# One ordered list instead of two for the head and the first feed-forward of a macaron block

## The chip, the cores and the metric

The kernel runs on one core of a Trainium2 chip. The core has a matrix engine (TensorE, PE in the profile), a vector engine (VectorE, DVE), a scalar engine (ScalarE, ACT), GpSimd (POOL) and SyncE (SP), which issues most of the transfers. The metric is the device time of one execution in microseconds (us), the median of several.

## The reference

One block on 256 tokens of width 2048, all in float32: a SwiGLU feed-forward (width 5632), a mixer, and a second feed-forward, each with an RMS norm before and after it and a residual.

```python
def _swiglu(x, w_gate, w_up, w_down):
    return (jax.nn.silu(x @ w_gate) * (x @ w_up)) @ w_down
...
f = _swiglu(_rmsnorm(h, ln_ffn1_pre[l]), ffn1_gate[l], ffn1_up[l], ffn1_down[l])
h = h + MACARON_WEIGHT * _rmsnorm(f, ln_ffn1_post[l])
mx = _hybrid_mixer(_rmsnorm(h, ln_mix_pre[l]), w_in[l], ...)
h = h + _rmsnorm(mx, ln_mix_post[l])
f = _swiglu(_rmsnorm(h, ln_ffn2_pre[l]), ffn2_gate[l], ffn2_up[l], ffn2_down[l])
h = h + MACARON_WEIGHT * _rmsnorm(f, ln_ffn2_post[l])
```

The mixer projects its input by `w_in`, runs an RWKV-7 recurrence on one part and windowed means on another (`_pool_branch`, with small matrices `pool_w`), gates both and projects by `w_out`.

## The kernel before

**Products.** Every float32 product is made of three: each operand is split into a high half (a cast to fp32r) and a low half (the operand less its high half). `mm3` (L332 to L334) issues the three matmuls, high with high (named L332 in the profile), low with high, high with low. A weight tile of 128x1024 goes from DRAM into a buffer (SP), is cast to its high half `wH` on ACT (L308, L386, L639), and its low half `wL` is a subtraction on DVE (L309, L396, L644). High and low halves sit in rings of five buffers each, so DVE and ACT stay a few tiles ahead of PE. Other tiles come from a common pool of 33 buffers (`unit`).

**The head.** `head` is the start of the program: it loads the input x in 512-column pieces and the first 512 columns of the gate's weights, transposes x on PE (`tr`, L939), and makes the high half `xH` of the transposed input on ACT (L948) and its low half `xL` on DVE (L957). Its loop over 16 blocks k of the contraction does two `mm3` for each k (token halves 0 and 1, banks `mm_120` and `mm_121`), and at every second k turns the next piece of x and splits the next weight tile.

**The first feed-forward's list.** What follows, the rest of `ffn`, is collected in `Plan`: each operation is a node with an engine, a cost and its dependencies. `Plan.solve` orders the nodes by these costs, and `run` issues them in that order. It begins with `normed` (four joins of `xH` and `xL` to `nx`, L1249, then a scaling by the norm's factor and a new split) and the up-projection's first 512 columns (`fetch`, with the cast at L386 and the low half at L396).

**Who sets the order.** `manual_schedule` opens a list: what is issued inside it, on the engines named, keeps its order. `head` opens one for PE, ACT, DVE and SP; `run` opens one for these and POOL. Between two lists, and outside any, a scheduler that estimates times (`schedule_with_timeline_sim=True`) decides what goes first on an engine. The mixer's recurrence and its pool branch are such code: generators paced by `yield` and placed by that scheduler.

**The mixer, as far as it matters here.** `rwkv` runs twice, on two halves of the channels. For the first half: `shift` (L1502 on ACT, L1505 on DVE) mixes a token with the one before it (`zr`, with a scratch `zb`); transposes `pV` on PE and their copies (L1823, L1824 on ACT); transposes `pk` (L1831) and a product on DVE (L1832); `AR` and `BK`, operands of the recurrence, from L1857 to L1867 on DVE; and `pA` (L1881), the matmuls of `BK` with `AR`. In the names below `R` is one of 15 work tiles. `pool_mix` makes the small products `mc` (L901) with `pool_w`, evicted to `yb` (L1710 on ACT, L1711 on DVE). Between them stand the large products with `w_in`, which need their weight halves from L308 and L309.

Of the kernel before, what the change touches and what calls it, by code (L numbers as in the profile page):

```python
# [76 lines left out]
class Tok:  # L77


    def __init__(s, *res):  # L80
        s.res, s.of, s.left, s.end, s.n = res, None, 0, 0.0, 1
# [150 lines left out]
class Block:  # L232
    def __init__(s, tc, ctx):
        s.tc = tc
        s.nc = nc = tc.nc
        E = ctx.enter_context
        s.n = 0
        s.nxt = None
        s.late, s.after, s.chain_pow = [], [], None
        s.own_stats = False  # L240
        s.plan, s.ready = Plan(), {}
        s.cp = E(tc.tile_pool(name="cp", bufs=1))
        s.wp = E(tc.tile_pool(name="wp", bufs=3))
        s.up = E(tc.tile_pool(name="up", bufs=NUNITS))
        s.tp = E(tc.tile_pool(name="tp", bufs=TB))
        s.sp = E(tc.tile_pool(name="sp", bufs=4))
        s.dp = E(tc.tile_pool(name="dp", bufs=1, space=bass.MemoryType.DRAM))
        s.pm = E(tc.tile_pool(name="pm", bufs=4, space=PSUM))
        s.pt = E(tc.tile_pool(name="pt", bufs=4, space=PSUM))
        s.ident = s.const([P, P], "ident")  # L250
        make_identity(nc, s.ident)
        s.mhalf = s.const([P, 16], "mhalf")
        nc.gpsimd.memset(s.mhalf, -0.5)
# [22 lines left out]

    def run(s):

        E = mybir.EngineType
        with s.tc.manual_schedule(engines={E.PE, E.Activation, E.DVE, E.SP, E.Pool}):
            for n in s.plan.solve():
                n.fn()
            if not s.own_stats:
                s.stats()
        s.plan, s.ready = Plan(), {}
# [506 lines left out]
    def head(s, w, c0, KT, do, keep, xs):  # L794

        load, turn = xs
        w32 = {}

        def get(k, n):
            w32[k] = (n, s.get_w(w, k, n, c0, 512, own=True))  # L800

        def split(k):
            n, t = w32[k]
            keep(s.two(t, k, n, 512))
        E = mybir.EngineType
        with s.tc.manual_schedule(engines={E.PE, E.Activation, E.DVE, E.SP}):
            ps = s.psum("warm")
            for _ in range(WARM):
                s.nc.tensor.transpose(ps[:, :P], s.ident, s.ident)
            load(0, 0)  # L810
            load(1, 0)
            load(None, None)
            get(0, 1)
            get(1, 1)
            get(2, 1)
            get(3, 1)
            for c in range(1, 4):
                load(0, c)
                get(4 * c, 2)
                load(1, c)  # L820
                get(4 * c + 2, 2)
            split(0)
            turn(0, 0)
            split(1)
            turn(1, 0)
            split(2)
            split(3)
            for k in range(KT):
                do(k, 0)
                do(k, 1)  # L830
                if k % 2 == 0 and k + 4 < KT:
                    turn(k // 2 % 2, k // 4 + 1)
                    split(k + 4)

    def stats(s):
        while s.late:
            for f in s.late.pop(0):
                f()
# [123 lines left out]
    def turn(s, T1, h, src):  # L962

        dst = T1.rearrange("p (j h k c) -> p h k j c", j=4, h=2, k=4)[:, h]
        s.nc.vector.transpose(out=dst, in_=src.rearrange("p (k j c) -> p k j c", k=4, j=4))  # L965
# [1197 lines left out]
```

## Time and profile before

| | |
|---|---|
| median of 3 runs | 2007.45 us (2005.02 to 2007.62) |
| profiled execution | 2005.37 us, span 2003.7 us |
| busy in the span | PE 1990.0 us, DVE 1813.6, ACT 1224.3, POOL 410.0 |
| granted TensorE clock | 0.999 |
| moved | 472.36 MB, 236 GB/s in the mean |

The span runs from the first to the last instruction. In a timeline row the first number is the start, the second the duration, both in us; then come engine, line of the kernel, operation, output and inputs, shapes and count; a bracket gives the idle time in front of it on its engine and what ended that. Durations of matmuls that follow each other overlap, so their pace is read from the starts. A row of the waits gives the sum in us, the number of times and the longest. SPq is SP's queue of transfers. A row of stretches gives the length, the busy time of PE, weight loads, DVE, ACT and POOL with counts, then the granted clock, the share of the DMA engines and GB/s.

### The profile page before, as it was taken

What the parts mean: (1) busy time and instruction counts of PE and PEld (TensorE: products, weight loads), DVE (VectorE), ACT (ScalarE), POOL (GpSimd) and SP (SyncE); (2) the same over time, 40 slices, a digit from 0 to 9 for tenths busy, and PEclk for the clock granted to TensorE, in tenths of its full rate; (3) what the DMA queues carried; (4) which work ended last, traced back from release to release, by engine and by line L of the source; (5) the groups of instructions that cost most, each with busy time, mean ns of one, the idle gap of its engine ahead of it and who ended that gap; (6) DMA issues with size and microseconds to landing.
All of it is one profiled execution on the core that took longest, in us unless ns stands there. A gap on an engine that the chain in (4) does not pass through costs nothing.

```text
span 2003.7 us, 29050 instructions
## 1 busy us (share of the span) xinstructions
PE 1990.0 (99%) x9903; PEld 1644.7 (82%) x9903; DVE 1813.6 (91%) x2462; ACT 1224.3 (61%) x1631; POOL 410.0 (20%) x747
## 2 busy tenths in 40 slices
PE   9999999999999999999999999999999999999998
PEld 7888888888888888888788788888888888888886
DVE  6999999999999957799689678989999999999997
ACT  7566665676665566685466434575666656666563
POOL 2222231323000113412320111012222313230000
PEclk9999999999999999999999999999999999999999
DMA  9788798878778767757556547768888988876784
GB/s 341 226 268 270 216 304 271 254 238 257 211 229 272 264 191 210 206 174 219 147 168 189 169 158 262 263 226 276 265 269 254 276 259 244 258 242 207 232 284 158
DMA packets 253941, 472.36 MB, mean 236 GB/s; under 512 B 27363, under 2 KB 30816, under 8 KB 253792
## 3 DMA queue, kind: packets, MB, share of 16 engines
q1 hardware_dynamic: 213984, 400.89, 60.4%
q0 software_dynamic: 39520, 69.08, 15.3%
q8 instruction: 78, 1.28, 0.3%
q10 hardware_dynamic: 288, 0.52, 0.1%
q14 instruction: 71, 0.58, 0.1%
HBM read 445.45 MB, written 8.39 MB: 227 GB/s over the span
## 4 chain that ended last, share of the span: by engine, by line
PE 93%; DVE 3%; DMA 2%; issue 1%; ACT 0%; SPq 0%; DVEq 0%; POOLq 0%; POOL 0%; ACTq 0%
PE mm L332 25%; PE mm L334 24%; PE mm L333 24%; PE ms L333 5%; PE ms L334 5%; PE ms L332 5%; DMA w<-in_ffn_down_dram 1%; DVE wL L644 1%; PE tr L939 1%; DVE wL L396 1%; DMA w<-in_w_out_dram 0%; PE pA L1881 0%; DVE t L622 0%; PE mc L901 0%; DVE t L627 0%
## 5 line engine op out<-in xcount | busy, mean ns | idle before, releaser
L332 PE MATMUL mm<-wH,xH 128*128 128x512 f32 (+1 forms) x2008 | 784.3, 391 | 2.0 <-ACT wH L386 1.5
L334 PE MATMUL mm<-wH,xL 128*128 128x512 f32 (+1 forms) x2008 | 779.4, 388 | 0.1
L333 PE MATMUL mm<-wL,xH 128*128 128x512 f32 (+1 forms) x2008 | 779.3, 388 | 0.1
L332 PEld LDWEIGHTS mm<-wH,xH 128*128 128x128 f32 x2008 | 377.2, 188 | 80.9 <-ACT wH L386 1.9
L334 PEld LDWEIGHTS mm<-wH,xL 128*128 128x128 f32 x2008 | 377.0, 188 | 78.7 <-DVE xL L957 1.1
L333 PEld LDWEIGHTS mm<-wL,xH 128*128 128x128 f32 x2008 | 377.3, 188 | 75.7 <-DVE wL L309 0.4
L639 ACT CAST wH<-t 128x1024 fp32r<-128x1024 f32 x244 | 257.1, 1055 | 221.2 <-PE mm L334 121.0
L386 ACT CAST wH<-w 128x1024 fp32r<-128x1024 f32 x293 | 302.8, 1053 | 128.6 <-PE mm L334 100.8
L396 DVE TENSOR_TENSOR wL<-w,wH 128x1024 fp32r<-128x1024 f32 x293 | 351.9, 1227 | 13.8 <-ACT wH L386 12.5
L644 DVE TENSOR_TENSOR wL<-t,wH 128x1024 fp32r<-128x1024 f32 x244 | 295.7, 1234 | 10.9 <-ACT wH L639 10.2
L309 DVE TENSOR_TENSOR wL<-w,wH 128x1024 fp32r<-128x1024 f32 (+2 forms) x184 | 217.5, 1190 | 84.6 <-ACT wH L308 83.2
L308 ACT CAST wH<-w 128x1024 fp32r<-128x1024 f32 (+2 forms) x184 | 188.8, 1030 | 167.0 <-PE mm L334 147.5
L639 ACT CAST wH<-w 128x1024 fp32r<-128x1024 f32 x244 | 200.1, 837 | 109.7 <-PE mm L334 75.1
L982 POOL DMA_DIRECT2D x<-T x352 | 180.6, 608 | 389.6 <-DVE T L965 76.1
L644 DVE TENSOR_TENSOR wL<-w,wH 128x1024 fp32r<-128x1024 f32 x244 | 231.6, 966 | 0.9 <-ACT wH L639 0.9
L333 PE MATMUL ms<-wL,sH 128*128 128x512 f32 x312 | 121.5, 389 | 0.2 <-DVE wL L644 0.2
L332 PE MATMUL ms<-wH,sH 128*128 128x512 f32 x312 | 121.4, 389 | 0.0
L334 PE MATMUL ms<-wH,sL 128*128 128x512 f32 x312 | 121.4, 389 | 0.0
L617 POOL DMA_DIRECT2D t<-in_ffn_up_dram x48 | 59.8, 1256 | 230.8 <-DMA t<-in_ffn_up_dram 56.1
L631 DVE TENSOR_TENSOR t<-w,t 128x512 f32<-128x512 f32 x122 | 85.5, 701 | 0.5 <-DMA w<-in_ffn_down_dram 0.2
L627 DVE TENSOR_TENSOR t<-w,t 128x512 f32<-128x512 f32 x122 | 85.3, 700 | 0.3 <-DMA w<-in_ffn_down_dram 0.3
L622 DVE TENSOR_TENSOR t<-w,w 128x1024 f32<-128x1024 f32 x60 | 73.8, 1231 | 2.8 <-DMA w<-in_ffn_down_dram 2.8
(353 smaller groups left out, 2312.4 us busy)
## 6 DMA issues: line engine op xcount, KB each, us to landing
w<-in_w_in_dram SPq DMA_DIRECT2D x128, 512.0 KB, 4.3
w<-in_ffn_down_dram SPq DMA_DIRECT2D x104, 512.0 KB, 6.5
w<-in_ffn_up_dram SPq DMA_DIRECT2D x94, 512.0 KB, 6.0
w<-in_ffn_gate_dram SPq DMA_DIRECT2D x92, 512.0 KB, 6.6
w<-in_ffn_gate_dram SPq DMA_DIRECT2D x168, 256.0 KB, 5.5
w<-in_ffn_down_dram SPq DMA_DIRECT2D x130, 256.0 KB, 4.9
w<-in_ffn_up_dram SPq DMA_DIRECT2D x116, 256.0 KB, 5.9
t<-in_ffn_up_dram POOLq DMA_DIRECT2D x48, 512.0 KB, 8.4
```

The costliest lines, as they stand in the source:

```text
L308: s.nc.scalar.copy(vH, v)
L309: s.nc.vector.tensor_tensor(out=vL, in0=v, in1=vH.bitcast(F32), op=ALU.subtract)
L332: nc.tensor.matmul(ps, aH, bH, start=start, stop=False, skip_group_check=seeded)
L333: nc.tensor.matmul(ps, aH, bL, start=False, stop=False, skip_group_check=seeded)
L334: nc.tensor.matmul(ps, aL, bH, start=False, stop=stop, skip_group_check=seeded)
L386: nc.scalar.copy(x["H"], x["v"])
L396: nc.vector.tensor_tensor(out=x["L"], in0=x["v"], in1=x["H"].bitcast(F32), op=ALU.subtract)
L627: V.tensor_tensor(out=v["t24"][:, 0], in0=v["a"][:, 0], in1=v["t13"][:, 1], op=ALU.add)
L631: V.tensor_tensor(out=v["t24"][:, 1], in0=v["b"][:, 1], in1=v["t24"][:, 0], op=ALU.add)
L639: nc.scalar.copy(H, src)
L644: V.tensor_tensor(out=L, in0=src, in1=H.bitcast(F32), op=ALU.subtract)
L982: nc.gpsimd.dma_start(out=x[0][q * 32:q * 32 + 32, i], in_=src[i * 32:i * 32 + 32, q])
```

## The change

The list that `head` opens is not closed at its end. It is kept in `s.open`, and `run` goes on in it; where no list is open, `run` opens one as before. Both now name the same five engines, so POOL is in the head's list too. No operation is added, removed or altered.

```diff
-        s.plan, s.ready = Plan(), {}
+        s.plan, s.ready, s.open = Plan(), {}, None
...
+    def listed(s):
+        E = mybir.EngineType
+        return s.tc.manual_schedule(engines={E.PE, E.Activation, E.DVE, E.SP, E.Pool})
+
     def run(s):
 
-        E = mybir.EngineType
-        with s.tc.manual_schedule(engines={E.PE, E.Activation, E.DVE, E.SP, E.Pool}):
+        with s.open or s.listed():
+            s.open = None
             for n in s.plan.solve():
                 n.fn()
...
-        E = mybir.EngineType
-        with s.tc.manual_schedule(engines={E.PE, E.Activation, E.DVE, E.SP}):
+        stack = ExitStack()
+        stack.enter_context(s.listed())
+        with stack:
             ps = s.psum("warm")
...
+            s.open = stack.pop_all()
```

In the changed kernel the lines behind `__init__` stand 4 lower, those behind `head` 6 lower (L332 is L336, L957 is L963), and buffer numbers are smaller by 3. Apart from that the order of instructions differs in two places; SP's and POOL's is the same throughout, and so is PE's outside the first place.

**First place: the seam of the two lists, PE.** `mm_120` and `mm_121` are the head's banks, `mm_498` (now `mm_495`) is the up-projection's. Before, near the end of the head:

```order
L334 MATMUL mm_121<-wH_317,xL_96 128x512
L332 MATMUL mm_120<-wH_346,xH_97 128x512
L332 MATMUL mm_498<-wH_488,xH_91 128x512
L333 MATMUL mm_120<-wL_347,xH_97 128x512
L334 MATMUL mm_120<-wH_346,xL_98 128x512
L332 MATMUL mm_121<-wH_346,xH_97 128x512
```

And in the changed kernel, 24 rows later, at the head's end:

```order
L338 MATMUL mm_120<-wH_375,xL_98 128x512
L336 MATMUL mm_121<-wH_375,xH_97 128x512
L337 MATMUL mm_121<-wL_376,xH_97 128x512
L338 MATMUL mm_121<-wH_375,xL_98 128x512
L336 MATMUL mm_495<-wH_485,xH_91 128x512
L337 MATMUL mm_495<-wL_486,xH_91 128x512
L338 MATMUL mm_495<-wH_485,xL_92 128x512
```

The up-projection's first matmul stood among the head's; it now stands behind all of them, followed by its second.

**The same seam, DVE.** `wL_318` to `wL_376` are the head's weight low halves, `xL` the input's, `nx` the joins, `wL_489` (now `wL_486`) the up-projection's first low half. Before:

```order
L309 TENSOR_TENSOR wL_318<-w_45_161,wH_317 128x1024
L957 SCALAR_TENSOR_TENSOR xL_98<-tr_333,g_90,xH_97 128x128 x4
L1249 TENSOR_TENSOR nx_457<-xH_93,xL_94 128x1024
L1249 TENSOR_TENSOR nx_465<-xH_95,xL_96 128x1024
L1249 TENSOR_TENSOR nx_473<-xH_91,xL_92 128x1024
L309 TENSOR_TENSOR wL_347<-w_46_164,wH_346 128x1024
L957 SCALAR_TENSOR_TENSOR xL_98<-tr_362,g_90,xH_97 128x128 x4
L309 TENSOR_TENSOR wL_376<-w_47_167,wH_375 128x1024
L1249 TENSOR_TENSOR nx_481<-xH_97,xL_98 128x1024
L396 TENSOR_TENSOR wL_489<-w_121_459,wH_488 128x1024
```

Changed:

```order
L313 TENSOR_TENSOR wL_318<-w_45_161,wH_317 128x1024
L963 SCALAR_TENSOR_TENSOR xL_98<-tr_333,g_90,xH_97 128x128 x4
L313 TENSOR_TENSOR wL_347<-w_46_164,wH_346 128x1024
L963 SCALAR_TENSOR_TENSOR xL_98<-tr_362,g_90,xH_97 128x128 x4
L313 TENSOR_TENSOR wL_376<-w_47_167,wH_375 128x1024
L1255 TENSOR_TENSOR nx_454<-xH_93,xL_94 128x1024
L1255 TENSOR_TENSOR nx_462<-xH_95,xL_96 128x1024
L1255 TENSOR_TENSOR nx_470<-xH_91,xL_92 128x1024
L1255 TENSOR_TENSOR nx_478<-xH_97,xL_98 128x1024
L400 TENSOR_TENSOR wL_486<-w_121_456,wH_485 128x1024
```

Three joins went from ahead of the head's last two weight low halves to behind them. ACT's order at the seam is the same in both.

**Second place: the mixer's first half, ACT**, about 855 to 895 us into the span. Before:

```order
L308 CAST wH_8489<-w_1803_8487 128x512
L1502 ACTIVATE zb<-R_6933,cols_724 128x256
L1502 ACTIVATE zr_8002<-R_6933,omu 128x256
L1502 ACTIVATE zb<-R_6933,cols_724 128x256
L1502 ACTIVATE zr_8002<-R_6933,omu 128x256 x3
L1783 ACTIVATE R_6932<-R_6935 128x1024
L1870 CAST yH_6963<-ident 128x1
L308 CAST wH_8509<-w_1808_8507 128x512
L1824 COPY R_6945<-pV_8375 64x4x64
L1823 COPY R_6944<-pV_8375 64x4x64
L1823 COPY R_6944<-pV_8380 64x4x64
L1824 COPY R_6945<-pV_8380 64x4x64
```

Changed:

```order
L312 CAST wH_8486<-w_1803_8484 128x512
L312 CAST wH_8506<-w_1808_8504 128x512
L1830 COPY R_6942<-pV_8372 64x4x64
L1829 COPY R_6941<-pV_8372 64x4x64
L1829 COPY R_6941<-pV_8377 64x4x64
L1830 COPY R_6942<-pV_8377 64x4x64
L1508 ACTIVATE zb<-R_6930,cols_721 128x256
L1508 ACTIVATE zr_7999<-R_6930,omu 128x256
L1508 ACTIVATE zb<-R_6930,cols_721 128x256
L1508 ACTIVATE zr_7999<-R_6930,omu 128x256 x3
L1789 ACTIVATE R_6929<-R_6932 128x1024
L1876 CAST yH_6960<-ident 128x1
```

A cast and the four copies of the second pair of `pV` moved ahead of the shifts.

**The same place, DVE.** Before, from the weight low half of the pool branch on:

```order
L309 TENSOR_TENSOR wL_8490<-w_1803_8487,wH_8489 128x512
L1505 TENSOR_TENSOR zr_8002<-zr_8002,zb 128x256 x2
L1805 COPY R_6940<-n_1781_8317 128x1024
L1867 TENSOR_TENSOR R_6941<-zr_8002,R_6931 64x8x64
L309 TENSOR_TENSOR wL_8510<-w_1808_8507,wH_8509 128x512
L1505 TENSOR_TENSOR zr_8002<-zr_8002,zb 128x256 x2
L1867 TENSOR_TENSOR R_6942<-zr_8002,R_6931 64x8x64
L1867 TENSOR_TENSOR R_6943<-zr_8002,R_6931 64x8x64
L309 TENSOR_TENSOR wL_8538<-w_1817_8535,wH_8537 128x1024
L1832 TENSOR_TENSOR R_6934<-R_6934,pk_8425 128x512
```

Changed:

```order
L313 TENSOR_TENSOR wL_8487<-w_1803_8484,wH_8486 128x512
L313 TENSOR_TENSOR wL_8507<-w_1808_8504,wH_8506 128x512
L1511 TENSOR_TENSOR zr_7999<-zr_7999,zb 128x256
L1811 COPY R_6937<-n_1781_8314 128x1024
L1511 TENSOR_TENSOR zr_7999<-zr_7999,zb 128x256
L1873 TENSOR_TENSOR R_6938<-zr_7999,R_6928 64x8x64
L1511 TENSOR_TENSOR zr_7999<-zr_7999,zb 128x256
L1838 TENSOR_TENSOR R_6931<-R_6931,pk_8422 128x512
L313 TENSOR_TENSOR wL_8535<-w_1817_8532,wH_8534 128x1024
```

One addition of `zr`, two products L1867 (now L1873) and the low half `wL_8538` (now `wL_8535`), which stood ahead of the first product with `pk`, stand behind it now; the remaining rows up to the low half of the tile after next hold the same operations in another order.

## The prediction

> **What bounds the kernel now.** I read the page's first lines, then the waits of TensorE, then the timelines of the two places where the order of instructions differs.
>
> ```profile
> span 2003.7 us, 29050 instructions
> ...
> PE 1990.0 (99%) x9903; PEld 1644.7 (82%) x9903; DVE 1813.6 (91%) x2462; ACT 1224.3 (61%) x1631; POOL 410.0 (20%) x747
> ...
> PE mm L332 <- ACT wH L386: 1.5, 1, 1.5
> ...
> PE ms L333 <- DVE wL L644: 0.2, 1, 0.2
> ```
>
> PE is busy 99% of the span. Its waits, sorted by size, run from the 1.5 us of the first line shown to the 0.2 of the last, six lines in all. So time changes only where PE gets a gap or loses one, and a gap once made is not won back later: there is almost no later idle time to swallow it. The longest wait stands at the seam between the two lists.
>
> PE's timeline at the seam (start, duration, then the instruction):
>
> ```profile
> 27.84 0.40 PE L332 MATMUL mm<-wH,xH 128*128 128x512 f32 x1
> 29.73 0.50 PE L332 MATMUL mm<-wH,xH 128*128 128x512 f32 x1 [1.49 <-ACT wH L386]
> 30.35 0.50 PE L333 MATMUL mm<-wL,xH 128*128 128x512 f32 x1
> 30.69 0.39 PE L334 MATMUL mm<-wH,xL 128*128 128x512 f32 x1
> ...
> 35.48 0.39 PE L334 MATMUL mm<-wH,xL 128*128 128x512 f32 x1
> 35.70 0.39 PE L333 MATMUL mm<-wL,xH 128*128 128x512 f32 x1
> 35.93 0.39 PE L334 MATMUL mm<-wH,xL 128*128 128x512 f32 x1
> ```
>
> Starts matter here, since durations overlap: two starts are 0.23 apart when nothing waits (35.70 to 35.93). The row at 29.73 is the up-projection's first matmul, standing amid the head's. From 27.84 to 30.35 two steps took 2.51 where 0.46 would do: 2.05 us lost, 1.66 to the cast and 0.39 to the low half that the row at 30.35 uses.
>
> VectorE (DVE) and ScalarE (ACT) at the same place:
>
> ```profile
> 21.42 1.13 DVE L957 SCALAR_TENSOR_TENSOR xL<-tr,g,xH 128x128 fp32r<-128x128 f32 x4 [0.94 <-ACT xH L948]
> 24.64 1.12 DVE L957 SCALAR_TENSOR_TENSOR xL<-tr,g,xH 128x128 fp32r<-128x128 f32 x4 [0.95 <-ACT xH L948]
> 25.68 3.49 DVE L1249 TENSOR_TENSOR nx<-xH,xL 128x1024 f32<-128x1024 f32 x3
> 29.08 1.22 DVE L309 TENSOR_TENSOR wL<-w,wH 128x1024 fp32r<-128x1024 f32 x1
> 30.22 1.12 DVE L957 SCALAR_TENSOR_TENSOR xL<-tr,g,xH 128x128 fp32r<-128x128 f32 x4
> 31.25 1.22 DVE L309 TENSOR_TENSOR wL<-w,wH 128x1024 fp32r<-128x1024 f32 x1
> 32.39 1.22 DVE L1249 TENSOR_TENSOR nx<-xH,xL 128x1024 f32<-128x1024 f32 x1
> 33.52 4.63 DVE L396 TENSOR_TENSOR wL<-w,wH 128x1024 fp32r<-128x1024 f32 x4
> ```
> ```profile
> 26.65 1.15 ACT L948 ACTIVATE xH<-tr,g 128x128 fp32r<-128x128 f32 x4 [1.11 <-PE tr L939]
> 28.60 2.96 ACT L386 CAST wH<-w 128x1024 fp32r<-128x1024 f32 x3
> ```
>
> Here DVE has no idle time from 24.64 on. Its three joins (25.68) run while ACT makes the high half of the last input block (26.65); in the stages before, DVE idled 0.94 us for that.
>
> **Step 1, the seam.** The matmul goes behind the head's last, the joins behind the head's low halves. PE then runs the head without a gap: 24 steps of 0.23 from 27.84 bring the up-projection's first matmul at 33.3, its second at 33.55. That one reads a low half (L396). DVE now: the head's weight low half at 25.68, 1.14 to 26.82; it waits for ACT, which ends at 27.80 (26.65 + 1.15), so the input's low half runs from 27.84 to 28.88 (1.04, as from 24.64 to 25.68), the last weight low half to 30.02, four joins of 1.135 (three took from 25.68 to 29.08) to 34.56, then the first L396 to 35.78. PE waits from 33.55 to 35.83: 2.28 us. Before, this step began at 35.70. One restart spacing of 0.34 (30.35 to 30.69) instead of 0.23 adds 0.11. Result: PE is 0.24 us later than before. The wait is not removed, it changes its place. Bounds: -2.05, if DVE had a way to run the L396 earlier, to +0.6, if the restart takes several slow steps as at 29.73; I take +0.24, since every link has a row.
>
> DVE itself is 1.04 us late behind this (34.56 against 33.52). Idle time that absorbs it stands a few operations later, and what SyncE queues behind these low halves waits here:
>
> ```profile
> 44.92 1.23 DVE L396 TENSOR_TENSOR wL<-w,wH 128x1024 fp32r<-128x1024 f32 x1 [1.50 <-ACT wH L386]
> 48.13 1.23 DVE L1253 TENSOR_TENSOR nx<-nx,rsb 128x1024 f32<-128x1024 f32 x1 [1.98 <-ACT rsb L1217]
> ```
> ```profile
> SPq L294 <- DVE wL L396: 5.2, 2, 4.5
> ```
>
> The loads that SP holds until then go out about 1 us later, in an unchanged order; PE had no wait for a load in this feed-forward, so I cost them at nothing, covered by loads issued well ahead. POOL's list is unchanged, and including POOL in the head's list moves nothing, since the head issues nothing there.
>
> **Step 2, the mixer.** Nothing is written differently there, but the scheduler's estimate of time has moved, and it orders ACT and DVE otherwise near 858 to 890 us. PE's order there is the same.
>
> ```profile
> 858.71 0.51 ACT L1502 ACTIVATE zb<-R,cols 128x256 f32<-128x256 f32 x1
> 862.67 0.37 ACT L1824 COPY R<-pV 64x256 f32<-64x256 f32 x1
> ```
> ```profile
> 860.55 0.60 PE L1818 MATMUL pV<-ident,zv 128*128 128x128 f32 x4
> 866.91 1.03 PE L1831 MATMUL pk<-ident,R 128*128 128x128 f32 x8
> 867.70 0.48 PE L332 MATMUL mm<-wH,xH 128*128 128x512 f32 x1
> 879.09 0.39 PE L333 MATMUL mm<-wL,xH 128*128 128x512 f32 x1
> 887.11 2.41 PE L1881 MATMUL pA<-R,R 64*128 64x128 f32 x32
> ```
> ```profile
> 864.51 0.83 DVE L1505 TENSOR_TENSOR zr<-zr,zb 128x256 f32<-128x256 f32 x2 [1.02 <-ACT zb L1502]
> 865.37 1.39 DVE L1867 TENSOR_TENSOR R<-zr,R 64x512 f32<-64x512 f32 x2
> 866.78 1.23 DVE L309 TENSOR_TENSOR wL<-w,wH 128x1024 fp32r<-128x1024 f32 x1
> 867.93 1.28 DVE L1832 TENSOR_TENSOR R<-R,pk 128x512 f32<-128x512 f32 x2
> 876.26 2.35 DVE L309 TENSOR_TENSOR wL<-w,wH 128x1024 fp32r<-128x1024 f32 x2
> 886.73 0.69 DVE L1857 TENSOR_TENSOR R<-R,R 64x512 f32<-64x512 f32 x1
> ```
>
> Before, ACT began the shifts (zb, zr) at 858.71 and copied the second pV at 862.67. Now the pV copies come first, and they cannot run before PE's transposes end (860.55 + 0.60 = 861.15). ACT idles some 2 us, and the shifts begin at about 862.6 (four copies of up to 0.37). DVE, which needs them, idles too. It reaches L1832 only when the first of PE's two pk banks is there (half of 1.03 behind 866.91, and 0.24 from step 1: 867.7, against 867.93), but with work left over that was done by then before: one zr addition (half of 0.83), two L1867 (1.39) and one weight low half (1.14, the distance from 866.78 to 867.93), together 2.95. The list from L1832 to the low half at 876.26 is otherwise the same operations without idle time. So that low half starts at 876.26 + 2.95 - 0.2 = 879.0 and ends at 880.2; PE wants it at 879.09 + 0.24. That is a first gap of 0.8. The same lag stays on DVE up to L1857, which ends at 887.42 before (886.73 + 0.69) and at 890.2 now. PE's pA, at 887.11, already waited for it to the tenth. So PE is 2.8 us later than before from there on, step 1's 0.24 included, in two or three gaps of which the last is the largest (about 1.9). Bounds: +0.24, if ACT finds the pV ready and nothing lags, to +3.5, if the pA's copies, which now stand behind one more cast on ACT, hold up a bank too. I take 2.8, since DVE's sum decides and its durations are all rows.
>
> **Sum.** 2005.37 (profiled execution: span 2003.7 and 1.7 around it) + 2.8 = 2008.2. The median shown, 2007.45, is 2.1 higher; the four executions known lie from 2005.02 to 2007.62, two near each end. Their mean, 2006.4, plus 2.8 gives the forecast 2009.2. A change under 0.2% (4.0 us) can hardly be told from none here, so the likeliest verdict is no change.
>
> **Rivals.** (a) The seam's wait is removed and nothing takes its place, and the mixer's lag is hidden: 2005.4 - 2.05 = 2003.3. For it speaks the 1.0 us that the first low half had in hand before (ready at 33.52 + 1.22 = 34.74, used at 35.70); against it, that DVE has 1.04 more ahead of it and PE comes 2.05 earlier. (b) Only step 2 is hidden: 2005.6. For it speaks that such rows often have slack; against it, that pA had none. (c) Slower: a gap is long enough that PE's clock is taken down afterwards. Rows for its price:
>
> ```profile
> 8.62 0.63 PE L332 MATMUL mm<-wH,xH 128*128 128x512 f32 x1
> 9.05 0.50 PE L333 MATMUL mm<-wL,xH 128*128 128x512 f32 x1
> ```
> ```profile
> 24.00:30.00 6.00, 4.51 (x22) 3.35 (x20) 5.37 (x8) 4.89 (x11) 0.00 (x0) 1.00 1.05 387
> ```
>
> In the first microseconds two starts lie 0.43 apart (8.62 to 9.05) instead of 0.23, and this lasts to about 10 us. A stretch of some 5 us at that pace loses 2.4 us, so one such gap gives 2005.4 + 2.8 + 2.4 = 2010.6, which is over 0.2%. Against it: the stretch with the 1.49 us gap keeps a granted clock of 1.00. It decides from the gap's length: 2.28 at the seam and about 1.9 at pA are longer than the one seen.
> The Trainium skill (TensorE: Matmul & The Clock Gate, Part 1) says that the clock falls to half after an idle window of about 3.4 us; by that, gaps of 2.3 us leave it alone and the rival gets less, and the row with 1.00 agrees as far as it goes.
>
> (d) The change does nothing: a few rows move and every wait ends when it did. This reads as no change as well.
>
> **Chances.** Forecast 0.55, (a) 0.08, (b) or (d) 0.22, (c) 0.12, the rest (buffers of the common pool are handed out in another order, so that a load may wait longer) 0.03. Slower by over 0.2%: (c), the rest, and the forecast's upper end with an unlucky set of executions, 0.05: 0.20. Faster: (a) is 2 us and reaches it only with luck: 0.05. Within: 0.75. The range runs from halfway between (a) and (b) on the lowest execution (2003.3 and 2005.02 + 0.24: 2004.3) to (c) on the mean of the executions, 2006.4 + 5.2, and a little over: 2011.8. The forecast's own range is 2007.0 to 2011.0, step 2's bound of 3.5 on the higher executions at the top.
>
> **What would show it.** In the timeline of PE after: no gap at 27.84, and one of about 2.3 us in front of the matmul with the first L396 low half, near 33.5. In DVE's: four joins in a row after the head's last low half, and 0.95 idle for ACT before them. Near 861 ACT idle for pV, and PE gaps just before 880 and at pA, near 888 to 890. The forecast is wrong if pA starts within 1 us of 887, or if PE's distance between starts after a gap stays at 0.43.

## The result and the profile after

| | before | after |
|---|---|---|
| median, 17 runs each | 2006.59 us (2004.80 to 2008.81) | 2010.59 us (2009.59 to 2012.62) |
| ratio | | 1.0022, 95% interval [1.0014, 1.0029] |

The change costs 4.0 us; 2.8 were forecast. The page of the profiled execution (2011.31 us), its span and busy times:

```profile
span 2009.6 us, 29049 instructions
...
PE 1991.6 (99%) x9903; PEld 1646.8 (82%) x9903; DVE 1813.5 (90%) x2462; ACT 1224.2 (61%) x1631; POOL 409.8 (20%) x747
```

PE's waits in the changed kernel (instruction, what it waited for; sum in us, times, longest):

```profile
PE mm L337 <- DVE wL L400: 2.1, 1, 2.1
PE tr L945 <- DMA x<-in_x_dram: 1.8, 1, 1.8
...
PE pA L1887 <- DVE R L1863: 1.2, 2, 1.1
PE pB L1906 <- DVE R L1898: 1.1, 2, 0.8
PE mm L336 <- ACT sgb L1523: 0.6, 1, 0.6
```

The wait for the up-projection's cast is gone. In its place stand one for the low half of L400 and three in the mixer (pA, pB and a bank that `sgb` evicts). The wait of `tr` for the input is at the program's start and scatters: in the other profiled executions, of all kernels, it lies between 0.3 and 1.7 us.

The seam, PE's timeline and then VectorE's (start, duration):

```profile
30.33 0.40 PE L336 MATMUL mm<-wH,xH 128*128 128x512 f32 x1
...
35.79 0.39 PE L336 MATMUL mm<-wH,xH 128*128 128x512 f32 x1
38.30 0.51 PE L337 MATMUL mm<-wL,xH 128*128 128x512 f32 x1 [2.12 <-DVE wL L400]
38.64 0.40 PE L338 MATMUL mm<-wH,xL 128*128 128x512 f32 x1
```
```profile
30.31 1.12 DVE L963 SCALAR_TENSOR_TENSOR xL<-tr,g,xH 128x128 fp32r<-128x128 f32 x4 [0.93 <-ACT xH L954]
...
32.48 4.62 DVE L1255 TENSOR_TENSOR nx<-xH,xL 128x1024 f32<-128x1024 f32 x4
37.02 4.63 DVE L400 TENSOR_TENSOR wL<-w,wH 128x1024 fp32r<-128x1024 f32 x4
```

From 30.33 to 35.79 PE steps without a gap. Then 2.51 us pass to the next start, 2.28 more than a step of 0.23: the low half that it needs stands behind four joins. Put row by row beside the profile of before, PE was already 2.46 us later in the head (the start's scatter; 2.45 to 2.49 by row), 0.21 later once the old gap was passed (30.56 against 30.35), and 2.75 later five starts behind the new gap (39.59 against 36.84). The seam so cost 2.75 - 2.46 = 0.29 net.

The mixer in the changed kernel: ACT, then VectorE, then PE.

```profile
863.51 0.62 ACT L312 CAST wH<-w 128x512 fp32r<-128x512 f32 x1 [1.94 <-PE mm L338]
864.04 0.36 ACT L1830 COPY R<-pV 64x256 f32<-64x256 f32 x1
...
865.33 0.51 ACT L1508 ACTIVATE zb<-R,cols 128x256 f32<-128x256 f32 x1
```
```profile
881.54 2.35 DVE L313 TENSOR_TENSOR wL<-w,wH 128x1024 fp32r<-128x1024 f32 x2
...
891.30 1.40 DVE L1863 TENSOR_TENSOR R<-R,R 64x512 f32<-64x512 f32 x2
...
894.54 3.50 DVE L313 TENSOR_TENSOR wL<-w,wH 128x1024 fp32r<-128x1024 f32 x3
...
898.34 1.22 DVE L313 TENSOR_TENSOR wL<-w,wH 128x1024 fp32r<-128x1024 f32 x1
899.48 0.41 DVE L1896 TENSOR_TENSOR R<-pA,mask 64x256 f32<-64x256 f32 x1
```
```profile
877.62 0.50 PE L336 MATMUL mm<-wH,xH 128*128 128x512 f32 x1 [0.59 <-ACT sgb L1523]
...
892.12 0.46 PE L1887 MATMUL pA<-R,R 64*128 64x128 f32 x2 [1.06 <-DVE R L1863]
892.75 2.05 PE L1887 MATMUL pA<-R,R 64*128 64x128 f32 x30 [0.17 <-DVE R L1863]
...
900.74 0.24 PE L1906 MATMUL pB<-ident,R 64*128 64x64 f32 x1 [0.27 <-DVE R L1898]
901.77 0.68 PE L1906 MATMUL pB<-ident,R 64*128 64x64 f32 x15 [0.79 <-DVE R L1898]
```

PE's lag against before grows in three steps: from 2.75 to 3.53 at the bank of `sgb`, over 3.87 (884.54 against 880.67) to 5.28 behind pA (894.73 against 889.45), and to 6.40 behind pB (902.38 against 895.98). The mixer so cost 6.40 - 2.75 = 3.65, and the seam and the mixer together 3.94. At the program's end PE's lag is 5.96, 0.44 less: near 1862 us the profile of before waits for a low half (the `ms` row of its waits) and loses time there. The third profile of before has no such wait, so this belongs to that execution and not to the change. At pB the evictions of pA (L1896, L1898) stand behind three low halves (894.54) and one more (898.34), which stood behind the first two pairs of them before.

### The profile page after: what moved, and what is told of

Read it like the earlier page. It is cut to its first block, busy times and chain, and to the rows that moved or that the text cites. A ratio compares the mean times of both kernels' runs of the same rounds, so it can differ in the third digit from the quotient of the medians.

```text
span 2009.6 us, 29049 instructions
## 1 busy us (share of the span) xinstructions
PE 1991.6 (99%) x9903; PEld 1646.8 (82%) x9903; DVE 1813.5 (90%) x2462; ACT 1224.2 (61%) x1631; POOL 409.8 (20%) x747
## 4 chain that ended last, share of the span: by engine, by line
PE 92%; DVE 3%; DMA 2%; issue 1%; ACT 0%; SPq 0%; DVEq 0%; POOLq 0%; POOL 0%; ACTq 0%
PE mm L336 24%; PE mm L338 24%; PE mm L337 24%; PE ms L337 5%; PE ms L336 5%; PE ms L338 5%; DMA w<-in_ffn_gate_dram 1%; DMA w<-in_ffn_down_dram 1%; DVE wL L400 1%; DMA w<-in_ffn_up_dram 0%; PE tr L945 0%; PE pA L1887 0%; DVE wL L648 0%; DVE wL L313 0%; DMA x<-in_x_dram 0%
## 5 line engine op out<-in xcount | busy, mean ns | idle before, releaser
L336 PE MATMUL mm<-wH,xH 128*128 128x512 f32 (+1 forms) x2008 | 785.7, 392 | 1.1 <-ACT sgb L1523 0.6
L336 PEld LDWEIGHTS mm<-wH,xH 128*128 128x128 f32 x2008 | 377.8, 188 | 79.6 <-ACT sgb L1523 1.0
L400 DVE TENSOR_TENSOR wL<-w,wH 128x1024 fp32r<-128x1024 f32 x293 | 350.9, 1223 | 13.3 <-ACT wH L390 11.9
L336 PE MATMUL ms<-wH,sH 128*128 128x512 f32 x312 | 121.5, 390 | 0.0
```

The source lines that it names most:

```text
L336: nc.tensor.matmul(ps, aH, bH, start=start, stop=False, skip_group_check=seeded)
L400: nc.vector.tensor_tensor(out=x["L"], in0=x["v"], in1=x["H"].bitcast(F32), op=ALU.subtract)
```

## The experiments

Theory: two terms that have nothing to do with each other, the seam (+0.3) and the mixer's other order (+3.65). Rival 1: the seam's gap costs everything. Rival 2: the program's start became slower, as the first profile seems to say.

**The two terms apart.** The change alters the order at the seam and in the mixer together, but small permutations of the one list alter them apart. `join` and `low` are marks that these kernels set on the nodes of the joins and of the up-projection's low halves; `run` then goes through `order`. Four kernels ran side by side, with 33 runs of the kernel before (median 2007.15 us). The first permutes only the four joins among their own places:

```diff
+        order = s.plan.solve()
+        if s.open:
+            at = [i for i, n in enumerate(order) if hasattr(n, "join")][:4]
+            joins = [order[i] for i in at]
+            for i, j in zip(at, [3, 0, 1, 2]):
+                order[i] = joins[j]
...
```

The two others put the joins behind the fifth or the sixth low half of the up-projection (`late5`, `late6`; the same lines with 5 for 6):

```diff
+        order = s.plan.solve()
+        if s.open:
+            joins = [n for n in order if hasattr(n, "join")][:4]
+            at = [n for n in order if hasattr(n, "low")][6-1]
+            order = [n for n in order if n not in joins]
+            i = order.index(at) + 1
+            order[i:i] = joins
...
```

> The one list, with only the four joins permuted among their own four places. PE's order and the seam stay as in the changed kernel; the mixer's order on DVE and ACT is that of the kernel before. Theory (two separate terms, seam +0.3, mixer +3.65): the gap of about 2.1 us ahead of the first L400 low half stays, pA starts with no lag of its own, and the time is the kernel before's +0.3 (2006.9 against 2006.6), 3.65 below the changed kernel. Rival 1 (the seam's gap costs everything, the mixer's rows had slack): +4.0, as the changed kernel. Rival 2 (the program's start, where the profile showed the changed kernel 2.46 us behind, is slower because the list is longer): +2.5 or more, with PE's first transposes late again.

> The one list, with the four joins moved behind the fifth low half of the up-projection; the mixer's order is that of the changed kernel. Theory: the seam's gap goes (2.12 of waiting and 0.11 of restart, against 0.3 net before: -2.0 to the kernel before), the mixer's +3.65 stays: +1.6, so 2008.2, 2.4 below the changed kernel. Rival 1 (all at the seam): the same time as late6. Rival 2 (the start): +0.5 or more, in late6 too. A further rival: the joins, 5.7 us later, hold up the norm and PE gets a gap after the first 512 columns of the up-projection; then both late5 and late6 lose some us again near 45 to 60 us.

> The one list, with the four joins moved behind the sixth low half of the up-projection; the mixer's order is that of the kernel before. Theory: neither the seam's gap nor the mixer's lag: -2.0 to the kernel before, 2004.6, and 3.65 below late5, from which it differs at the seam by one place only. Rival 1 (all at the seam): equal to late5. Rival 2 (the start): +0.5 or more.

> The changed kernel once more, for comparison on the same chip. Theory: +4.0 to the kernel before (seam +0.3, mixer +3.65). Its start should scatter as that of the other kernels: if PE's first matmul at full pace comes at 10 to 11 us here, the 2.46 us by which it came later in the first profile were that execution's own. Rival 2: it comes at 13 us or later again.

| kernel | seam's gap | mixer's order | median, us (11 runs) | to before | ratio, 95% interval |
|---|---|---|---|---|---|
| after_again | yes | changed | 2010.59 | +3.4 | 1.0019 [1.0010, 1.0028] |
| joins_order | yes | as before | 2006.38 | -0.8 | 0.9998 [0.9990, 1.0007] |
| late5 | no | changed | 2007.56 | +0.4 | 1.0008 [0.9999, 1.0017] |
| late6 | no | as before | 2004.05 | -3.1 | 0.9988 [0.9979, 0.9997] |

The mixer's order is worth 4.2 us with the gap (2010.59 - 2006.38) and 3.5 without it (2007.56 - 2004.05); the gap 2.3 and 3.0. So the terms add within the scatter, and rival 1 falls. The runs of the kernel before scatter over 4.1 us here, so a difference of medians moves easily: by the ratios the four rows are +3.8, -0.4, +1.6 and -2.4 us. Expected were +4.0, +0.3, +1.6 and -2.0. Rival 2 falls too: in the profile of after_again PE's head ran level with that of before (0.10 us later at its second transpose, against 1.15 in the first profile), and in that of after_4, taken later, it was 0.18 earlier at the head's end, where the first profile was 2.49 later. That after_again took nearly the same time as the first profile (2010.59 against 2011.31 us) does not show this by itself: it lost some 1.5 us in another way, told below under the pace.

PE's waits in joins_order, the two longest from the seam on, and in late6, all that there are:

```profile
PE mm L343 <- DVE wL L406: 2.1, 1, 2.1
...
PE mm L342 <- DVE u L713: 0.5, 1, 0.5
...
```
```profile
PE warm L823 <- POOL ident masks.py:199: 1.4, 1, 1.4
PE mm L343 <- DVE u L716: 0.5, 1, 0.5
PE ms L344 <- DVE wL L657: 0.4, 1, 0.4
PE tr L954 <- DMA x<-in_x_dram: 0.3, 1, 0.3
PE pU L1993 <- DVE R L2018: 0.3, 1, 0.3
```

With the old order in the mixer, pA, pB and `sgb` do not appear; with the joins late, the seam does not appear either. The joins of late6 (L1264) run behind six low halves, eleven us after the first of them:

```profile
30.36 3.49 DVE L407 TENSOR_TENSOR wL<-w,wH 128x1024 fp32r<-128x1024 f32 x3
...
41.30 4.79 DVE L1264 TENSOR_TENSOR nx<-xH,xL 128x1024 f32<-128x1024 f32 x4
```

late6 beats both kernels: 3.1 us under the one before and 6.5 under the changed one. late5 differs at the seam too, by 0.35: there the copy `rb` stands behind the joins and PE waits 0.18 for it. A join's place among four so decides the order of another stage 830 us later. What carries it there is read from the programs only: the buffers of the common pool are handed out in another order from the norm on, and the scheduler comes to another order in the mixer. Which of its estimates tips it was not tried.

**Has pB slack?** The kernel before, with a product on VectorE done twice between pA's release and the evictions of pA:

```diff
-                V.tensor_tensor(out=g8(BK[q], h), in0=gr(a[R, i2]), in1=gr(ilam[R, i2]),
-                                op=ALU.mult)
+                for _ in range(2 if hf == 0 and q == 1 else 1):
+                    V.tensor_tensor(out=g8(BK[q], h), in0=gr(a[R, i2]), in1=gr(ilam[R, i2]),
+                                    op=ALU.mult)
```

> The kernel before, with the product BK of the second half of heads (L1857, two rows of 0.61 us between starts on VectorE) done twice, with the same values; the only change of order is these two rows more, behind the one that releases pA and ahead of the evictions of pA. Theory (pB has no slack: in the changed kernel one more low half of 1.14 us stood ahead of the evictions and pB came 1.1 later): pA starts as before, PE waits some 1.2 us in front of pB, nothing is given back, +1.2 us. Rival (VectorE's idle time takes it up, pB was late in the changed kernel only because pA was): no wait at pB, 0.

VectorE's two added rows, and PE at pA and pB:

```profile
893.06 1.39 DVE L1858 TENSOR_TENSOR R<-R,R 64x512 f32<-64x512 f32 x2
894.48 0.42 DVE L1891 TENSOR_TENSOR R<-pA,mask 64x256 f32<-64x256 f32 x1
```
```profile
887.11 2.38 PE L1882 MATMUL pA<-R,R 64*128 64x128 f32 x32
895.75 0.24 PE L1901 MATMUL pB<-ident,R 64*128 64x64 f32 x1 [0.59 <-DVE R L1893]
896.79 0.68 PE L1901 MATMUL pB<-ident,R 64*128 64x64 f32 x15 [0.80 <-DVE R L1893]
```

pA starts where it did, pB waits 0.59 and 0.80, and PE is 1.49 us later behind it than in the third profile of before (897.40 against 895.91) and stays so to the end. The ratio is 1.0009 [1.0000, 1.0018], some 1.8 us; the medians, 2008.24 against 2005.78, differ by 2.5, and the profiled execution (2006.50 us) is one of the shortest. 1.2 were expected. The two rows took more than that: the first eviction starts at 894.48 here and at 893.07 in the kernel before, 1.41 later. pB has no slack: what goes ahead of pA's evictions on VectorE is paid in full, as the low half of 1.14 us in the changed kernel was.

**Has pA slack?** The same edit with `q == 0 and h == 0` for `q == 1`:

> The kernel before, with one product BK of the first half of heads (L1857, 0.61 us between starts) done twice, with the same values, ahead of the row that releases pA; by it the scheduler also puts one weight low half (1.14 us) from behind the evictions of pA to ahead of them, as in the changed kernel. Theory: pA waits 0.6 and pB another 1.1 in front of it, +1.7 us in all, as the changed kernel's pA and pB did on top of each other. Rival 1 (pA has slack): pB alone, +1.1. Rival 2 (pB takes up its wait): +0.6 alone.

Measured 2013.61 us (5 runs) against 2005.78, ratio 1.0038 [1.0025, 1.0050]: +7.8, where 1.7 were expected. VectorE and PE:

```profile
889.96 3.50 DVE L309 TENSOR_TENSOR wL<-w,wH 128x1024 fp32r<-128x1024 f32 x3
893.38 0.68 DVE L1858 TENSOR_TENSOR R<-R,R 64x512 f32<-64x512 f32 x1
```
```profile
894.11 3.78 PE L1882 MATMUL pA<-R,R 64*128 64x128 f32 x32 [6.17 <-DVE R L1858]
```

I had taken the added row to stand ahead of pA's release. It took the releasing row's place, and that row went behind three low halves, where it ends at 894.06. So it is another experiment than the one meant, yet it answers the question: pA starts at 894.11, as soon as this row ends, and nothing of its wait is won back. And pA itself took 3.78 instead of 2.40: PE ran at a lower pace behind this gap of 6.2 us (from 891.04 to 897.87 the granted clock is 0.50). That is the next point.

**The pace behind a gap.** In the profile of after_again PE did not go on at 0.23 between starts behind the seam's gap:

```profile
33.43 0.39 PE L336 MATMUL mm<-wH,xH 128*128 128x512 f32 x1
35.95 0.50 PE L337 MATMUL mm<-wL,xH 128*128 128x512 f32 x1 [2.12 <-DVE wL L400]
...
37.10 0.63 PE L338 MATMUL mm<-wH,xL 128*128 128x512 f32 x1
37.53 0.63 PE L336 MATMUL mm<-wH,xH 128*128 128x512 f32 x1
```

From about 36.8 to 40.2 the starts are 0.43 apart, and the granted clock is 0.50. To see whether the kernel before has it too, and what decides it, kernels already known ran again for their profiles:

> The kernel before once more, for a second profile of its start and seam. In one profile of the changed kernel PE ran at half pace (0.43 us between starts) from 36.9 to 40.2 us behind a gap of 2.3 us, in the other profile with the same gap it did not. Theory W: the pace is decided in stretches of about 3.4 us that run on from the program's start whatever happens; a stretch with much idle time (2.3 of 3.4 us sufficed, 1.45 did not) is followed by one at half pace, which costs some 1.5 us. The kernel before, with 1.66 and 0.39 us lost at the seam, then shows it in some executions, where both fall into one stretch: those of 2007 us and more have it, those of 2005 have not. Rival: the executions of 2007 us and more differ at the start alone (the input's transfer, the time at which full pace begins).

> The kernel before a third time, for the same question: by theory W a profile of 2007 us or more has seven or eight starts in a row 0.43 us apart behind the seam's gap, one of 2005 us none; by the rival neither has them.

> The changed kernel a third time, for the pace behind the seam's gap. Theory W: the pace is decided in stretches of 3.41 us that run on without regard to the work; a stretch with more than some 1.7 to 2.0 us of idle time is followed by one stretch at half pace. The time at which full pace begins in the head gives the phase; from it, the seam's gap of 2.3 us either lies within one stretch (then eight or so starts 0.43 apart begin at its end, and the execution is some 1.5 us longer) or is cut by a boundary into parts of under 1.5 us (then none). Rival: the pace falls at a fixed time behind the gap's begin, whatever the phase.

> As after_3, for another phase: theory W tells from the time at which full pace begins whether PE slows down behind the gap, the rival that it does so always or never.

> The one list with the four joins permuted, once more: the same gap of 2.3 us at the seam, for a further phase. Theory W and the rival as for after_3. The mixer again shows no wait at pA and pB.

The second profile of before (2007.54 us), from the head's change to full pace to the end of the slow stretch:

```profile
10.87 0.75 PE L332 MATMUL mm<-wH,xH 128*128 128x512 f32 x1
11.45 0.41 PE L333 MATMUL mm<-wL,xH 128*128 128x512 f32 x1
...
28.64 0.39 PE L332 MATMUL mm<-wH,xH 128*128 128x512 f32 x1
30.52 0.50 PE L332 MATMUL mm<-wH,xH 128*128 128x512 f32 x1 [1.49 <-ACT wH L386]
...
31.94 0.61 PE L333 MATMUL mm<-wL,xH 128*128 128x512 f32 x1
...
35.33 0.41 PE L332 MATMUL mm<-wH,xH 128*128 128x512 f32 x1
```

The same profile in stretches (the number behind the counts is the granted clock):

```profile
4.64:8.05 3.41, 1.78 (x11) 1.19 (x11) 1.25 (x4) 2.21 (x7) 0.00 (x0) 1.00 0.99 366
8.05:11.46 3.41, 3.40 (x10) 2.21 (x11) 3.41 (x10) 2.24 (x7) 1.83 (x4) 0.50 1.04 396
...
28.53:31.94 3.41, 1.81 (x8) 0.93 (x7) 3.41 (x7) 3.41 (x5) 0.00 (x0) 1.00 1.05 386
31.95:35.36 3.41, 3.41 (x10) 2.63 (x9) 3.41 (x4) 2.86 (x9) 0.00 (x0) 0.50 1.06 386
```

The third (2004.90 us) has the same wait of 1.49 and no slow start. Full pace begins near 11.3 in the second; six stretches of 3.41 (the length of the slow one in the granted clock, 31.95 to 35.36) further is 31.8, where the slow pace begins, and it lasts to 35.3. The table has all profiles with a gap at the seam. The end of the stretch is worked out from the time at which the head changes to full pace (from the spacing of starts, to about 0.2 us). The heads of the last four ran at full pace from the first matmul; there the time is that at which full clock begins in the trace's record of the granted clock.

| profile | full pace from | n x 3.41 later | idle in the gap, before and behind that time | half pace |
|---|---|---|---|---|
| before_2 | 11.3 | 31.8 (n = 6) | 2.0 and 0 | 31.9 to 35.3 |
| after_again | 9.6 | 36.9 (8) | 2.3 and 0 | 36.8 to 40.2 |
| after_3 | 10.8 | 34.7 (7) | 0.5 and 1.8 | none |
| after (first) | 13.5 | 37.4 (7) | 1.4 and 0.9 | none |
| joins_order | 12.7 | 36.6 (7) | 1.0 and 1.3 | none |
| before (first) | 9.2 | 29.7 (6) | 1.6 and 0.4 | none |
| pA_late, at the seam | 10.3 | 30.8 (6) | 1.7 and 0.4 | none |
| after_4 | 5.7 | 36.4 (9) | 2.3 and 0 | 36.4 to 39.8 |
| joins_order_2 | 4.9 | 35.6 (9) | 2.2 and 0.1 | 35.6 to 39.0 |
| before_3 | 4.5 | 28.4 (7) | 0.4 and 1.7 | none |
| pB_late | 4.7 | 28.6 (7) | 0.5 and 1.5 | none |

The executions took 2010.61 us (after_4), 2006.84 (joins_order_2) and 2009.45 (after_3). The slow pace begins between 0.1 us ahead of the gap's end and 1.4 behind it, so the rival of a fixed delay falls. At the seam theory W holds in all eleven: idle time of 2.0 us or more within one stretch brings a stretch at half pace, 1.8 or less does not.

The program's start shows that idle time is not the whole condition. In before_2 the first stretch at full clock, 4.64 to 8.05, is followed by one at half pace as well (above). before_3 was busy for even less of its first, and went on at full clock:

```profile
4.49:7.90 3.41, 1.72 (x11) 1.06 (x11) 1.27 (x4) 2.04 (x6) 0.00 (x0) 1.00 1.01 360
7.91:11.32 3.41, 2.93 (x13) 1.93 (x13) 3.41 (x10) 3.02 (x10) 1.74 (x4) 1.00 1.06 401
```

These stretches hold transposes and a few large matmuls, where those at the seam hold large matmuls nearly alone. What else counts there is not known, so 2.0 us is a figure for this seam and not a rule.

A slow stretch costs 1.4 us (before_2: PE's lag against the first profile of before goes from 0.96 to 2.35) to 1.6 (after_4: from -0.04 to 1.68, of which 0.15 come without it). Three of six profiles with the gap of 2.3 us have it, and one of five with the seam of the kernel before (pA_late and pB_late among them). It may be part of why late6, which has no such gap, gains 3.1 by the median where 2.0 were expected, and why its runs spread over 1.6 us only (2003.34 to 2004.92) and those of before over 4.1. That is not shown: late5 has no such gap either, and its runs spread over 2.9 (2007.24 to 2010.12, the longest being the profiled one, which has no slow stretch behind its start). How often each kernel has it, and so its share in the 4.0 us, cannot be told from so few profiles.

## Why the prediction was right, and where its size was off

- **The head's gap goes, and its place is taken.** As forecast: 2.28 us lost in front of the first L400 low half, with four joins in a row ahead of it and 0.93 of idle time for ACT before. Net +0.29 for +0.24; the restart gave 0.11 and later rows some more.
- **VectorE's lag and SP's loads behind the seam, costed at nothing.** PE has no wait for either, and its lag stays at 2.75 from 39.59 to the mixer.
- **The mixer up to pA.** The low half came at 881.54 for 876.26, 2.53 later once the 2.75 are taken off; the prediction's 879.0 is 2.5 later once step 1 is. Behind pA the mixer's part of the lag is 5.28 - 2.75 = 2.53, forecast 2.56. Two readings in it were off without effect: ACT's idle time before the pV copies ends with a buffer of the ring that PE releases for the cast ahead of them (863.51), not with pV; and most of the gap "just before 880" stands 2 to 3 us earlier, at the bank that `sgb` evicts late (0.78).
- **The mixer behind pA: the term that was mis-sized.** Step 2 let PE be 2.8 us later "from there on". pB took another 1.12 (6.40 - 5.28). The prediction had something of the kind in its upper bound only, as copies of pA behind one more cast on ACT (+0.7); it was the low half that belongs to this cast, on VectorE, ahead of pA's evictions. pB_late shows that nothing at pB absorbs it.
- **The sum.** 0.29 + 3.65 = 3.94 beside 4.0 measured. The base was right: 2006.4 for 2006.59. Of the 1.4 us between the forecast 2009.2 and the median 2010.59, pB is 1.1. Rival (c)'s 2010.6 is the measured median by coincidence: it starts from one execution of 2005.4 us and adds 2.4 for a slow stretch that, in the first profile, did not come.
- **No change or slower.** The prediction held no change the likeliest, drawing the line at 0.2%. The medians differ by 0.2%, and the interval, [1.0014, 1.0029], lies on both sides of that line, so on which side the time fell is luck. The interval excludes 1, however: with 17 runs each, a change of 4 us can be told from none.
- **Rivals.** (a), (b) and (d) did not happen. (c) happens in part: a slow stretch stands behind the gap in half of the profiles, at 1.4 to 1.6 us and not 2.4. But the kernel before pays it too in some executions, and most of the 4.0 us is there without it: in after_3, which has no slow stretch, PE's lag still goes from 0.75 at the seam to 4.49 behind pB. The row with a clock of 1.00 that spoke against (c) was from an execution in which a boundary cut the gap; and it ends at 30.00, 0.27 us behind the gap, where in before_2 the slow stretch began 1.4 us behind it. So it could not speak for or against. By the prediction's own sign (starts that stay 0.43 apart after a gap) the forecast's account was incomplete for after_again and after_4, and it held for after_3 and the first profile. The Trainium skill (TensorE: Matmul & The Clock Gate, Part 1) calls the window free-running, and the phases above agree; its idle window of about 3.4 us as the condition does not: 2.0 to 2.3 us sufficed here.

## What to carry to other kernels

Joining two ordered lists removes a wait only if the order at the joint is right too: the same one list gave +3.4 or -3.1 us, by the place of four joins of 1.1 us each. After such an edit compare the order of every stage, not only the one edited, and follow a moved row to every later matmul that reads behind it on its engine: pA's release was followed, the evictions behind it were not. In this kernel a wait of PE of 1.5 to 2.1 us could cost 1.5 us more than its length; at the seam whether it did was a matter of phase, so one profile does not show it.

## What the runs showed of the hardware

In the profiles PE's pace changed only in steps of about 3.4 us that ran on whatever the work did: at 9.5, 36.8 and 40.3 us in after_again, eight stretches and one apart. At the seam, idle time of 2.0 to 2.3 us within one stretch was followed by one at half pace (granted clock 0.50, starts 0.43 apart for 0.23); 1.8 us or less was not. At the start as much idle time was followed by half pace in before_2 and by full pace in before_3.

Executions of one kernel differ by 2 to 4 us. A slow stretch is worth 1.4 to 1.6 of that. The start gives another part: PE waited 0.3 to 1.8 us for the input, full clock began between 4.5 and 13.6 us, and PE's lag at the head's end, against the first profile of before, lay between -0.2 and 2.5 us.
